# Row standard deviation on one Trainium2 core: another assignment of rows to partitions, single-row loads, and last rows loaded in parts

## The chip, the cores and the metric

One core of one Trainium2 chip runs the kernel; the other cores are idle. Times are device microseconds of one execution, lower is better. A profile's span (first to last instruction) is about 2 us shorter than the time of the same execution. An execution is called slow here when it took over 1.5% more than the fastest one of the same kernel.

DVE is the vector engine and ACT the scalar engine; SP only issues loads and stores. A load is carried out by 16 DMA engines in *packets*; a packet of a load is here the contiguous piece that goes to one partition. A load *lands* when its last byte is in place.

## The reference

```python
x = np.random.randn(8192, 8192).astype(np.float32)     # 268.4 MB

def reference(x):
    return np.std(x, axis=1)                           # 8192 values
```

Each number is read once and used twice, in a sum and in a sum of squares. The variance is (sum of squares - sum^2 / N) / N.

## The kernel before

There are 128 partitions and 8192 rows, so each partition gets 64 rows. Before the change, partition p gets the 64 consecutive rows from 64p on: rows read at the same time by neighbouring partitions lie 64 x 32 KiB = 2 MiB apart. I call that distance the *pitch*. A tile holds two rows of each partition: 8.4 MB, one contiguous piece of 64 KB per partition.

```python
K = 2
T = R // (P * K)                                        # 32 tiles
xv = x.rearrange("(p t k) m -> t p k m", p=P, t=T, k=K)
xpool = ...tile_pool(name="xtiles", bufs=3)
...
for t in range(T):
    xt = xpool.tile([P, K, C], mybir.dt.float32)
    nc.sync.dma_start(out=xt[:], in_=xv[t])             # L39
    nc.vector.reduce_sum(out=allsum[:, t, :], in_=xt[:], axis=...)      # L41, DVE
    for k in range(K):
        for s in range(S):                              # two halves of a row, ACT
            nc.scalar.activation(out=dummy[:], in_=xt[:, k, s*CS:(s+1)*CS],
                                 func=Square, accum_out=allsq[:, t, k, s:s+1])
# after the loop: reduce allsq, square of the sums, subtract (DVE), Sqrt (ACT), one store
nc.sync.dma_start(out=out.rearrange("(p i) -> p i", p=P), in_=std)
```

Of the kernel before, what the change touches and what calls it, by code (L numbers as in the profile page):

```python
# [1 line left out]

# [4 lines left out]


@with_exitstack  # L10
def kernel(
    ctx: ExitStack,
    tc: tile.TileContext,
    x: bass.AP,
    out: bass.AP,
):
    nc = tc.nc
    P = nc.NUM_PARTITIONS
    R, C = x.shape
    K = 2  # L20
    T = R // (P * K)
    S = 2
    CS = C // S
    N = float(C)
    inv_n = 1.0 / N

    xv = x.rearrange("(p t k) m -> t p k m", p=P, t=T, k=K)

    xpool = ctx.enter_context(tc.tile_pool(name="xtiles", bufs=3))
    stats = ctx.enter_context(tc.tile_pool(name="stats", bufs=1))  # L30
    psum = ctx.enter_context(tc.tile_pool(name="psumdump", bufs=1, space=bass.MemoryType.PSUM))

    dummy = psum.tile([P, CS], mybir.dt.float32)
    allsum = stats.tile([P, T, K], mybir.dt.float32)
    allsq = stats.tile([P, T, K, S], mybir.dt.float32)

    for t in range(T):
        xt = xpool.tile([P, K, C], mybir.dt.float32)
        nc.sync.dma_start(out=xt[:], in_=xv[t])  # L39

        nc.vector.reduce_sum(  # L41
            out=allsum[:, t, :],
            in_=xt[:],
            axis=mybir.AxisListType.X,
        )

        for k in range(K):
            for s in range(S):
                nc.scalar.activation(  # L49
                    out=dummy[:],  # L50
                    in_=xt[:, k, s * CS:(s + 1) * CS],
                    func=mybir.ActivationFunctionType.Square,
                    accum_out=allsq[:, t, k, s:s + 1],
                )

    sq = stats.tile([P, T * K], mybir.dt.float32)
    nc.vector.reduce_sum(out=sq, in_=allsq, axis=mybir.AxisListType.X)  # L57

    m2 = stats.tile([P, T * K], mybir.dt.float32)
    nc.vector.scalar_tensor_tensor(  # L60
        out=m2,
        in0=allsum,
        scalar=inv_n,
        in1=allsum,
        op0=mybir.AluOpType.mult,
        op1=mybir.AluOpType.mult,
    )
    nc.vector.tensor_sub(sq, sq, m2)  # L68
    std = stats.tile([P, T * K], mybir.dt.float32)
    nc.scalar.activation(  # L70
        out=std,
        in_=sq,
        func=mybir.ActivationFunctionType.Sqrt,
        scale=inv_n,
    )
    nc.sync.dma_start(out=out.rearrange("(p i) -> p i", p=P), in_=std)


# [1 line left out]
_INS = ['x']  # L80
_OUTS = [((8192,), 'float32')]


# [23 lines left out]
```

## Time and profile before

The time at prediction was 659.8 us (three runs). The profile on which the prediction was made has a span of 662.7 us. Its execution took 664.8 us.

| part of the span | us | what runs |
|---|---|---|
| start | 1.2 | nothing to compute on yet |
| load stream | 641.2 | 32 loads, back to back |
| tail | 20.3 | reduce of the last tile, small operations, store |

From the page of the kernel before: busy time by engine; then, in 40 slices of the span, the busy tenths of the DMA engines and the rate in GB/s; then the costliest group (busy us, mean ns; idle before and what ended it) and the issue line (median us from issue to landing).

```profile
DVE 551.6 (83%) x35; ACT 477.6 (72%) x259; POOL 0.2 (0%) x4
DMA  8999999999999999999999999999999999999950
GB/s 316 340 396 403 396 431 439 388 439 412 407 443 443 439 411 415 443 443 419 415 431 443 443 431 392 443 444 407 415 443 443 443 431 396 439 443 439 392 245 2
L41 DVE TENSOR_REDUCE allsum<-xt 128x2 f32<-128x16384 f32 x32 | 551.0, 17220 | 108.6 <-DMA xt<-in_x_dram 108.6
xt<-in_x_dram SPq DMA_DIRECT2D x32, 41.5
```

The DMA row is 9 from the second slice to the end of the stream, and what ended DVE's idle time is always a load: the kernel is bound by the load stream. Yet the rate is not even. The engines are about as busy in the first two slices as later, but move 316 and 340 GB/s, against 425 on the mean of the other slices of the stream (388 to 444). The same in windows of 21 us (window, its length, busy time and instructions of DVE, ACT and GpSimd, clock, busy share of DMA, GB/s):

```profile
0.00:21.00 21.00, 0.00 (x0) 1.28 (x1) 0.20 (x4) 1.00 0.95 331
21.00:42.00 21.00, 13.58 (x1) 13.49 (x7) 0.00 (x0) 1.00 0.94 346
42.00:63.00 21.00, 15.97 (x2) 13.53 (x9) 0.00 (x0) 1.00 1.02 409
105.00:126.00 21.00, 17.48 (x2) 15.09 (x9) 0.00 (x0) 1.00 1.05 437
```

The chain of waits in order of time (start us, us, what) gives the two ends of the span:

```profile
1.17 49.47 DMA xt<-in_x_dram
67.94 45.04 DMA xt<-in_x_dram
...
601.03 41.32 DMA xt<-in_x_dram
...
642.37 17.22 DVE allsum L41
659.59 0.19 DVE sq L57
```

The chain's second load lands at 67.94 + 45.04 = 113.0 us; it is the fifth of all. The last load lands at 642.4 us. Then DVE spends 17.2 us on a tile on which nothing could start earlier.

### The profile page before, as it was taken

What the parts mean: (1) busy time and instruction counts of PE and PEld (TensorE: products, weight loads), DVE (VectorE), ACT (ScalarE), POOL (GpSimd) and SP (SyncE); (2) the same over time, 40 slices, a digit from 0 to 9 for tenths busy, and PEclk for the clock granted to TensorE, in tenths of its full rate; (3) what the DMA queues carried; (4) which work ended last, traced back from release to release, by engine and by line L of the source; (5) the groups of instructions that cost most, each with busy time, mean ns of one, the idle gap of its engine ahead of it and who ended that gap; (6) DMA issues with size and microseconds to landing.
All of it is one profiled execution on the core that took longest, in us unless ns stands there. A gap on an engine that the chain in (4) does not pass through costs nothing.

```text
span 662.7 us, 432 instructions
## 1 busy us (share of the span) xinstructions
DVE 551.6 (83%) x35; ACT 477.6 (72%) x259; POOL 0.2 (0%) x4
## 2 busy tenths in 40 slices
DVE  0279787898888898888899888889888889988888
ACT  0268666787667788767778777678877777877777
POOL 0000000000000000000000000000000000000000
DMA  8999999999999999999999999999999999999950
GB/s 316 340 396 403 396 431 439 388 439 412 407 443 443 439 411 415 443 443 419 415 431 443 443 431 392 443 444 407 415 443 443 443 431 396 439 443 439 392 245 2
DMA packets 4754, 268.49 MB, mean 405 GB/s; under 512 B 656, under 2 KB 656, under 8 KB 656
## 3 DMA queue, kind: packets, MB, share of 16 engines
q1 hardware_dynamic: 4752, 268.47, 96.2%
q14 instruction: 2, 0.02, 0.0%
HBM read 268.44 MB, written 0.03 MB: 405 GB/s over the span
## 4 chain that ended last, share of the span: by engine, by line
DMA 71%; DVE 29%; issue 0%; SPq 0%; ACT 0%
DMA xt<-in_x_dram 71%; DVE allsum L41 29%; SPq L39 0%; ACT std L70 0%; DVE sq L68 0%; DVE sq L57 0%; DVE m L60 0%
## 5 line engine op out<-in xcount | busy, mean ns | idle before, releaser
L41 DVE TENSOR_REDUCE allsum<-xt 128x2 f32<-128x16384 f32 x32 | 551.0, 17220 | 108.6 <-DMA xt<-in_x_dram 108.6
L49 ACT ACTIVATE dummy<-xt 128x4096 f32<-128x4096 f32 x128 | 459.2, 3587 | 180.6 <-DMA xt<-in_x_dram 177.6
L49 ACT ACTIVATION_READ_ACCUMULATOR dummy<-xt 128x1 f32 x128 | 23.8, 186 | 0.0
L49 ACT ACT_TABLE_LOAD x1 | 1.3, 1283 | 0.7 <-PEq L91 0.7
L70 ACT ACTIVATE std<-sq 128x64 f32<-128x64 f32 x1 | 0.3, 256 | 1.5 <-DVE sq L68 1.5
L70 ACT ACT_TABLE_LOAD x1 | 1.3, 1283 | 0.0
L57 DVE TENSOR_REDUCE sq<-allsq 128x64 f32<-128x128 f32 x1 | 0.3, 276 | 0.0
L68 DVE TENSOR_TENSOR sq<-sq,m 128x64 f32<-128x64 f32 x1 | 0.2, 224 | 0.0
L60 DVE SCALAR_TENSOR_TENSOR m<-allsum 128x64 f32<-128x64 f32 x1 | 0.2, 217 | 0.0
L91 POOL MEMSET const-bfloat16-1.0<- 128x1 bf16 x1 | 0.1, 101 | 0.0
L91 POOL MEMSET const-uint8-127<- 128x1 uint8 x1 | 0.1, 101 | 0.0
L91 POOL MEMSET const-float32-0.0<- 128x1 f32 x1 | 0.1, 98 | 0.2 <-issue 0.2
L91 POOL MEMSET const-float32-1.0<- 128x1 f32 x1 | 0.1, 98 | 0.0
## 6 DMA issues: line engine op xcount, KB each, us to landing
xt<-in_x_dram SPq DMA_DIRECT2D x32, 41.5
out_dram<-std SPq DMA_DIRECT2D x1, 32.0 KB, 1.5
```

Of the source, the lines that this page charges most:

```text
L41: nc.vector.reduce_sum(out=allsum[:, t, :], in_=xt[:], axis=mybir.AxisListType.X,)
L49: nc.scalar.activation(out=dummy[:], in_=xt[:, k, s * CS:(s + 1) * CS], func=mybir.ActivationFunctionType.Square, accum_out=allsq[:, t, k, ...
L57: nc.vector.reduce_sum(out=sq, in_=allsq, axis=mybir.AxisListType.X)
L60: nc.vector.scalar_tensor_tensor(out=m2, in0=allsum, scalar=inv_n, in1=allsum, op0=mybir.AluOpType.mult, op1=mybir.AluOpType.mult,)
L68: nc.vector.tensor_sub(sq, sq, m2)
L70: nc.scalar.activation(out=std, in_=sq, func=mybir.ActivationFunctionType.Sqrt, scale=inv_n,)
L91: nc = _bacc.Bacc("TRN2", target_bir_lowering=False, num_devices=1)
```

## The change

The intent has two parts. The tail: load one row per partition at a time, and the last ten rows in halves and quarters, so that little work is left after the last byte. The layout: group the rows by 16 (`G`), so that the pitch is 16 x 32 KiB = 512 KiB. Further, the results of the first 48 rows are finished early, partly on GpSimd.

```diff
-    xv = x.rearrange("(p t k) m -> t p k m", p=P, t=T, k=K)
+    G = 16
+    xg = x.rearrange("(g p r) m -> g r p m", p=P, r=G)
+    xrows = [xg[i // G, i % G] for i in range(I)]          # I = 64
+    out_pi = out.rearrange("(g p r) -> p g r", p=P, r=G)
+    NB = I - G
+    for i in range(I):
+        n = 1 if i < I - 10 else 2 if i < I - 4 else 4
+        rows.append((i, [C * j // n for j in range(n + 1)]))
-    xpool = ... bufs=3          # tiles of two rows
+    xpool = ... bufs=5          # tiles of one row
...
+    def do_row(i, cuts):
+        xt = xpool.tile([P, C], FP32, name="xt")
+        for ci in range(len(cuts) - 1):
+            c0, c1 = cuts[ci], cuts[ci + 1]
+            nc.sync.dma_start(out=xt[:, c0:c1], in_=xrows[i][:, c0:c1])
+            nc.vector.reduce_sum(out=asum[:, i - base, ci:ci + 1], in_=xt[:, c0:c1], ...)
+            ...  # Square with accum_out, in pieces of at most half a row
...  # after row 47: sums and squares of rows 0 to 47 combined on GpSimd into vA
...  # after row 63: the same for the last 16 rows on DVE into vB
+    stdA = Sqrt(vA);  nc.sync.dma_start(out=out_pi[:, 0:NB // G], in_=stdA...)
+    stdB = Sqrt(vB);  nc.scalar.dma_start(out=out_pi[:, NB // G:], in_=stdB...)
```

More of the change, by code (lines that the diff above doesn't have):

```diff
@@ L7 @@
 from concourse._compat import with_exitstack
+FP32 = mybir.dt.float32
 @with_exitstack
@@ L19 @@
     R, C = x.shape
-    K = 2
-    T = R // (P * K)
-    S = 2
-    CS = C // S
+    I = R // P
     N = float(C)
     inv_n = 1.0 / N
-    xv = x.rearrange("(p t k) m -> t p k m", p=P, t=T, k=K)
-    xpool = ctx.enter_context(tc.tile_pool(name="xtiles", bufs=3))
+    CS = C // 2
+    G = 16
[3 more added lines that the diff above has]
+    NB = I - G
+    rows = []
+    for i in range(I):
+        n = 1 if i < I - 10 else 2 if i < I - 4 else 4
+        rows.append((i, [C * j // n for j in range(n + 1)]))
@@ L30 @@
+    xpool = ctx.enter_context(tc.tile_pool(name="xtiles", bufs=5))
     stats = ctx.enter_context(tc.tile_pool(name="stats", bufs=1))
     psum = ctx.enter_context(tc.tile_pool(name="psumdump", bufs=1, space=bass.MemoryType.PSUM))
-    dummy = psum.tile([P, CS], mybir.dt.float32)
-    allsum = stats.tile([P, T, K], mybir.dt.float32)
-    allsq = stats.tile([P, T, K, S], mybir.dt.float32)
-    for t in range(T):
-        xt = xpool.tile([P, K, C], mybir.dt.float32)
-        nc.sync.dma_start(out=xt[:], in_=xv[t])
-        nc.vector.reduce_sum(
-            out=allsum[:, t, :],
-            in_=xt[:],
-            axis=mybir.AxisListType.X,
-        )
-        for k in range(K):
-            for s in range(S):
+    dummy = psum.tile([P, CS], FP32)
@@ new lines @@
+    NT = I - NB
+    sumA = stats.tile([P, NB, 4], FP32)
+    sqA = stats.tile([P, NB, 4], FP32)
+    sumB = stats.tile([P, NT, 4], FP32)
+    sqB = stats.tile([P, NT, 4], FP32)
+    nc.vector.memset(sumB, 0.0)
+    nc.vector.memset(sqB, 0.0)
+    invn_t = stats.tile([P, 1], FP32)
+    nc.vector.memset(invn_t, inv_n)
+    def do_row(i, cuts):
+        asum, asq, base = (sumA, sqA, 0) if i < NB else (sumB, sqB, NB)
+        xt = xpool.tile([P, C], FP32, name="xt")
+        for ci in range(len(cuts) - 1):
+            c0, c1 = cuts[ci], cuts[ci + 1]
+            nc.sync.dma_start(out=xt[:, c0:c1], in_=xrows[i][:, c0:c1])
+            nc.vector.reduce_sum(
+                out=asum[:, i - base, ci:ci + 1],
+                in_=xt[:, c0:c1],
+                axis=mybir.AxisListType.X,
+            )
+            nsub = (c1 - c0 + CS - 1) // CS
+            step = (c1 - c0) // nsub
+            for si in range(nsub):
+                s0 = c0 + si * step
@@ L49 @@
                 nc.scalar.activation(
-                    out=dummy[:],
-                    in_=xt[:, k, s * CS:(s + 1) * CS],
+                    out=dummy[:, 0:step],
+                    in_=xt[:, s0:s0 + step],
                     func=mybir.ActivationFunctionType.Square,
-                    accum_out=allsq[:, t, k, s:s + 1],
+                    accum_out=asq[:, i - base, ci + si:ci + si + 1],
                 )
-    sq = stats.tile([P, T * K], mybir.dt.float32)
-    nc.vector.reduce_sum(out=sq, in_=allsq, axis=mybir.AxisListType.X)
@@ L59 @@
-    m2 = stats.tile([P, T * K], mybir.dt.float32)
-    nc.vector.scalar_tensor_tensor(
-        out=m2,
-        in0=allsum,
-        scalar=inv_n,
-        in1=allsum,
-        op0=mybir.AluOpType.mult,
-        op1=mybir.AluOpType.mult,
-    )
-    nc.vector.tensor_sub(sq, sq, m2)
-    std = stats.tile([P, T * K], mybir.dt.float32)
-    nc.scalar.activation(
-        out=std,
-        in_=sq,
-        func=mybir.ActivationFunctionType.Sqrt,
-        scale=inv_n,
-    )
-    nc.sync.dma_start(out=out.rearrange("(p i) -> p i", p=P), in_=std)
+    vA = stats.tile([P, NB], FP32)
@@ new lines @@
+    for (i, cuts) in rows:
+        do_row(i, cuts)
+        if i == NB - 1:
+            tsqA = stats.tile([P, NB], FP32)
+            nc.gpsimd.tensor_add(tsqA, sqA[:, :, 0], sqA[:, :, 1])
+            t0 = stats.tile([P, NB], FP32)
+            nc.gpsimd.tensor_mul(t0, sumA[:, :, 0], sumA[:, :, 0])
+            nc.gpsimd.tensor_mul(t0, t0, invn_t.to_broadcast((P, NB)))
+            nc.gpsimd.tensor_sub(vA, tsqA, t0)
+    tsqB = stats.tile([P, NT], FP32)
+    nc.vector.reduce_sum(out=tsqB, in_=sqB, axis=mybir.AxisListType.X)
@@ new lines @@
+    tsumB = stats.tile([P, NT], FP32)
+    nc.vector.reduce_sum(out=tsumB, in_=sumB, axis=mybir.AxisListType.X)
+    m2 = stats.tile([P, NT], FP32)
+    nc.vector.scalar_tensor_tensor(
+        out=m2, in0=tsumB, scalar=inv_n, in1=tsumB,
+        op0=mybir.AluOpType.mult, op1=mybir.AluOpType.mult,
+    )
+    vB = stats.tile([P, NT], FP32)
+    nc.vector.tensor_sub(vB, tsqB, m2)
+    stdA = stats.tile([P, NB], FP32)
+    nc.scalar.activation(out=stdA, in_=vA,
+                         func=mybir.ActivationFunctionType.Sqrt, scale=inv_n)
@@ L80 @@
+    nc.sync.dma_start(out=out_pi[:, 0:NB // G], in_=stdA.rearrange("p (g r) -> p g r", r=G))
+    stdB = stats.tile([P, NT], FP32)
+    nc.scalar.activation(out=stdB, in_=vB,
+                         func=mybir.ActivationFunctionType.Sqrt, scale=inv_n)
+    nc.scalar.dma_start(out=out_pi[:, NB // G:], in_=stdB.rearrange("p (g r) -> p g r", r=G))
 _INS = ['x']
```

## The prediction

> **What bounds the kernel now.** The load stream. In the chain of waits, DMA of xt and the DVE reduce of xt alternate (71% and 29%), but the reduce stands there only because it frees a buffer: a load is issued when a buffer comes free and lands a median 41.5 us later (issue table), about twice its own 19.4 us, so a second one is always queued, and the slices show DMA busy at 9 from the second on. DVE (83%) and ACT (72%) wait for data. The 662.7 us span falls into three parts (chain in order of time, timeline):
> - 0 to 1.2 us: the start.
> - 1.2 to 642.4 us: the stream, 641.2 us for 268.4 MB, 419 GB/s. Its 4096 packets of 64 KB take 2.42 us each once settled (434 GB/s on 16 engines). At that rate it would take 256 x 2.42 = 619 us, so 22 us are lost. 15 us of them go in the first five loads (landed at 113 us, against 97 us plus the start); the windows show 331 and 346 GB/s in the first two 21 us stretches, 409 in the next two, with the engines busy all the same: packets are slower, not fewer.
> - 642.4 to 662.7 us: the tail, 20.3 us: DVE reduces the whole last tile (17.2 us), small operations and sqrt (0.9 us), output DMA (2.2 us).
>
> **What the change does.**
> 1. Tail. The last rows are cut in quarters (128x2048). From 17220 ns for 16384 columns and 276 ns for 128, DVE takes about 2.3 us for one; ACT about 2.1 us, then the table load (1.28 us). Add four small DVE operations (0.8 us), sqrt (0.26 us), output DMA (2.2 us): about 6 us after the last byte. Gain about 14 us, all on the critical path.
> 2. Row layout. The partition pitch in memory falls from 2 MiB to 512 KiB. The Trainium skill, DMA: Bandwidth & Descriptors, section Latency and other measured facts, gives 164 GB/s at 2 MiB, 207 at 512 KiB, 214 when padded, and suspects lock-stepped streams meeting in the same memory channels. 164/214 is 77%; this trace's start is 331/434 = 76%, and the loss fades[...]. No run here shows the 512 KiB case yet; at 97% the first five loads should lose about 3 us. Estimated gain about 12 us.
> 3. Costs. Packets of 32 KB and less (about 10,500): if a packet has some 10 ns of fixed cost, 3 us; small chunks 1 us. Eighty-odd issues of 0.33 us on SP are hidden. DVE needs 8.7 to 9.2 us a row against 9.7 us of DMA, ACT 7.5; five 4 MB buffers leave at least three rows queued.
> 4. GpSimd's part and sqrt of the first 48 rows come before the end, off the path.
>
> **Prediction.** 659.8 - 14.2 - 12 + 3.5: about 637 us, range 629 to 648. Faster by over 2%: 0.85, within 2%: 0.12, slower: 0.03. The floor (stream at 434 GB/s, start, short tail, 2 us outside the span) is about 629 us.
>
> **What would show it right or wrong.** Last load to the end of the span: 5 to 8 us, not 20. First two 21 us windows above 400 GB/s; if they stay near 335, step 2 is wrong and the time is near 648. Settled time per 8.4 MB within 0.3 us of 19.5.
>
> **What could be wrong.** The 512 KiB pitch may keep streams in lock-step longer; small packets may cost more; the chunked loads of one tile might be made to wait for each other's readers, opening gaps in DMA over the last ten rows; the first loads may be slow for another reason than pitch.

## The result

The new kernel takes 635.88 us (median of 12 runs, 635.75 to 636.05). The old one, in 15 runs over several occasions, has a median of 659.67 us (653.79 to 675.07). The ratio of the fast runs is 0.9663 (95% interval 0.9641 to 0.9685): faster by 3.4%. Ratios here are the mean time of one kernel's fast runs over that of the other's of the same rounds, so they are not quite the ratios of the medians quoted. The runs of the new kernel lie within 0.3 us of each other; the 12 fast ones of the old kernel scatter by 7.6 us (653.79 to 661.41), and three more were slow.

The page after, the same lines (DVE's group is now that of the first 48 rows), and the issue line of the last store:

```profile
DVE 558.4 (88%) x89; ACT 480.0 (76%) x276; POOL 1.3 (0%) x8
DMA  8999999999999999999999999999999999999995
GB/s 366 436 432 438 430 432 430 434 430 430 432 432 432 432 430 432 430 430 436 432 430 436 432 429 432 432 432 432 430 436 428 430 430 422 430 429 425 421 422 204
L60 DVE TENSOR_REDUCE sumA<-xt 128x1 f32<-128x8192 f32 x48 | 416.9, 8686 | 61.5 <-DMA xt<-in_x_dram 61.5
xt<-in_x_dram SPq DMA_DIRECT2D x54, 4096.0 KB, 39.8
out_dram<-stdB ACTq DMA_DIRECT2D x1, 8.0 KB, 1.5
```

The windows after:

```profile
0.00:21.00 21.00, 7.72 (x4) 8.70 (x5) 0.20 (x4) 1.00 0.94 389
21.00:42.00 21.00, 18.53 (x3) 14.84 (x8) 0.00 (x0) 1.00 1.00 431
588.00:609.00 21.00, 20.41 (x9) 18.16 (x17) 0.00 (x0) 1.00 1.01 421
```

The chain of waits after, its end:

```profile
608.34 19.90 DMA xt<-in_x_dram
...
628.26 0.03 DVE sumB L60
628.29 2.17 issue
630.46 0.21 DVE tsqB L89
```

The slow start is gone: the second window moves 431 GB/s instead of 346. The rate is flat, and sags to 421 only at the end, where packets are small. The last load lands at 628.2 us, and the span ends 5.9 us later instead of 20.3 us. The "0.03" and "2.17 issue" together are the DVE reduce of the last quarter row.

A profile of an ordinary execution of the old kernel (experiment w1, on another chip) has its last load at 634.6 us and a span of 655.0 us. Against that one, the 20.9 us that the new span is shorter are 14.5 us of tail and 6.4 us of stream. Against the first profile (664.8 us, a slow execution) it would look like 14.4 and 14.1 us; the excess belongs to that slow execution.

### The profile page after: what moved, and what is told of

It reads as the page before. It is cut to its first block, busy times and chain, and to the rows that moved or that the text cites. A ratio compares the mean times of both kernels' runs of the same rounds, so it can differ in the third digit from the quotient of the medians.

```text
span 634.1 us, 643 instructions
## 1 busy us (share of the span) xinstructions
DVE 558.4 (88%) x89; ACT 480.0 (76%) x276; POOL 1.3 (0%) x8
## 4 chain that ended last, share of the span: by engine, by line
DMA 84%; DVE 15%; issue 0%; SPq 0%; ACT 0%
DMA xt<-in_x_dram 84%; DVE sumA L60 14%; DVE sumB L60 1%; SPq L59 0%; ACT stdB L105 0%; DVE tsqB L89 0%; DVE vB L98 0%; DVE m L93 0%; DVE tsumB L91 0%
## 5 line engine op out<-in xcount | busy, mean ns | idle before, releaser
L69 ACT ACTIVATE dummy<-xt 128x4096 f32<-128x4096 f32 (+1 forms) x136 | 460.6, 3386 | 148.8 <-DMA xt<-in_x_dram 146.8
L60 DVE TENSOR_REDUCE sumA<-xt 128x1 f32<-128x8192 f32 x48 | 416.9, 8686 | 61.5 <-DMA xt<-in_x_dram 61.5
L60 DVE TENSOR_REDUCE sumB<-xt 128x1 f32<-128x2048 f32 (+2 forms) x34 | 140.6, 4165 | 10.5 <-DMA xt<-in_x_dram 10.5
L69 ACT ACTIVATION_READ_ACCUMULATOR dummy<-xt 128x1 f32 x136 | 25.3, 186 | 0.0
```

What stands on the lines that cost most here:

```text
L60: nc.vector.reduce_sum(out=asum[:, i - base, ci:ci + 1], in_=xt[:, c0:c1], axis=mybir.AxisListType.X,)
L69: nc.scalar.activation(out=dummy[:, 0:step], in_=xt[:, s0:s0 + step], func=mybir.ActivationFunctionType.Square, accum_out=asq[:, i - base, ...
```

## The experiments

The theory is that the slow start comes from the 2 MiB pitch, and that the gain is the cured stream plus the shorter tail. The rivals: the start was slow because of the large packets or the three 8 MB loads issued at once (*size*); the rows merely lay too far apart (*distance*); the cuts cost in the stream what they save in the tail. "Before" is always the old kernel run beside the experiment on the same chip.

### x1: the new kernel at the old pitch

```diff
-    G = 16
+    G = 64          # pitch 2 MiB; output views adapted
```

> The new kernel with the old row layout: row pitch between partitions 2 MiB again (64 rows), everything else (single rows of 32 KB packets, five buffers, cut last rows) as after the change. Theory pitch: the slow start comes back, the first two 21 us windows read about 330 to 350 GB/s, the time rises by 10 to 15 us to 646 to 651 us and the runs scatter by several us again. Rival size: the start was slow because of 64 KB packets or three 8 MB loads at once; then this stays near 636 us and the first windows above 385 and 430.

Measured: 663.31 us (661.91 to 663.99) beside 653.21 for before, ratio 1.0153 (1.0132 to 1.0174). The expectation missed: it is not 10 to 15 but 27 us slower than the new kernel, and 1.5% slower than the kernel before. The loss also sits elsewhere. Windows of x1:

```profile
0.00:21.00 21.00, 7.12 (x4) 8.18 (x4) 0.20 (x4) 1.00 0.90 356
21.00:42.00 21.00, 17.91 (x3) 15.31 (x10) 0.00 (x0) 1.00 1.00 426
567.00:588.00 21.00, 17.68 (x4) 14.84 (x8) 0.00 (x0) 1.00 1.01 411
588.00:609.00 21.00, 15.69 (x6) 13.46 (x11) 0.00 (x0) 1.00 0.99 296
630.00:651.00 21.00, 11.64 (x6) 10.01 (x10) 0.00 (x0) 1.00 1.01 263
```

The start is nearly healthy (426 in the second window). The halved and quartered rows at the end run at 411, then at 296 and 263 GB/s, with the engines fully busy. The 8 KB packets took 465 ns at the median, against 313 ns after the change. So the pitch does matter, but what it costs depends on how long the pieces are. My reading of the slow start as a property of the pitch alone was too simple.

### x2: the old kernel at the new pitch

```diff
-    xv = x.rearrange("(p t k) m -> t p k m", p=P, t=T, k=K)
+    xg = x.rearrange("(g p t k) m -> g t p k m", p=P, k=K, t=8)   # pitch 512 KiB
+    xv = [xg[t // 8, t % 8] for t in range(T)]
```

> The old kernel (pairs of rows, 64 KB packets, 8 MB loads, three buffers, uncut tail) with the new layout alone, pitch 512 KiB. Theory pitch: stream about 621 us instead of 641, second window above 425 GB/s, time about 644 us with a scatter below 1 us, tail still 20 us. Rival size: time near 659 us and the first windows near 335.

Measured: 646.49 us (646.35 to 646.56), ratio 0.9898 (0.9881 to 0.9916). Windows and the chain's end of x2:

```profile
0.00:21.00 21.00, 0.00 (x0) 1.28 (x1) 0.20 (x4) 1.00 0.94 399
21.00:42.00 21.00, 17.22 (x1) 14.84 (x8) 0.00 (x0) 1.00 1.02 443
```

```profile
582.83 40.74 DMA xt<-in_x_dram
...
623.59 17.22 DVE allsum L43
```

With 64 KB packets, 8 MB loads and three buffers all kept, the slow start vanishes and so does the scatter (four runs within 0.2 us, seven of before within 2.6). The rival *size* falls: large packets alone do no harm. The time is 2.5 us over the expected 644: the stream took 622.4 us instead of 621 and the tail 20.7 instead of 20; the rest is rounding. Beside its own before (653.21), the layout alone is worth 6.7 us. The last load lands at 623.6 us: these 622.4 us are close to the 619 us that 256 packets of 2.42 us per engine need.

### x3: a pitch of 63 rows

Is it the distance, or the power of two? With a pitch of 63 rows (2 MiB less 32 KiB), 63 loads cover the first 8064 rows, and one load takes the last 128.

```diff
-    xg = x.rearrange("(g p r) m -> g r p m", p=P, r=G)          # G = 16
+    G = I - 1
+    xg = x[0:P * G].rearrange("(p r) m -> r p m", p=P)
+    xrows = [xg[i] for i in range(G)] + [x[P * G:]]
```

> The new kernel with a pitch of 63 rows (2 MiB less 32 KiB) for 63 of its 64 loads, and the last 128 rows as one load of pitch one row. Theory aliasing: what hurts is a pitch at a large power of two, so this is as fast as after the change, 635 to 637 us, second window above 425 GB/s. Rival distance: what hurts is that the rows read at one time lie megabytes apart; then it is as slow as with 2 MiB, 646 to 651 us.

Measured: 641.84 us (641.65 to 642.15), ratio 0.9827 (0.9812 to 0.9842). That fits neither number, but the profile parts it cleanly. The chain's end, and the issue lines of the output stores of x3:

```profile
608.20 19.84 DMA xt<-in_x_dram
628.05 0.02 issue
```

```profile
out_dram<-stdB SPq DMA_DIRECT2D x1, 0.5 KB, 6.9
out_dram<-stdB ACTq DMA_DIRECT2D x1, 7.5 KB, 7.6
```

The last load lands at 628.05 us, as after the change (628.24), cut rows included. So rows almost 2 MiB apart are harmless: *distance* falls, and what hurts is a pitch at 2 MiB, or closer to it than 32 KiB. The missing 6 us are in the last stores: their runs are 60 and 4 bytes long here, and the larger landed 7.6 us after issue instead of 1.5. I had not thought of the output. All their packets had ended by 632.4 us, 1.1 us after issue; what the rest was spent on, which of the two stores was at fault, and whether the length of a run or its alignment matters, no run separates.

### x4: no row cut

```diff
-        n = 1 if i < I - 10 else 2 if i < I - 4 else 4
+        n = 1
```

> The new kernel with no row cut into parts. Theory tail: the last landing comes about 1 to 2 us earlier (no 8 KB packets), the tail from last landing to the end grows from 5.9 to about 12.3 us, so the time is about 640.5 to 641.5 us. Rival: the cuts cost in the stream what they save in the tail; then 636 us, with the last landing some 6 us earlier.

Measured: 640.68 us (640.60 to 640.85), as expected. The chain's end of x4:

```profile
586.53 40.50 DMA xt<-in_x_dram
...
627.05 0.04 DVE sumB L60
627.09 8.57 issue
```

Without cuts the last load lands 1.2 us earlier and DVE then needs 6.4 us more. So the cuts are worth 4.8 us (640.68 - 635.88; the spans differ by 5.0), and the rest of the tail's gain, 17.2 - 8.6 = 8.6 us of DVE time, comes from tiles of one row instead of two.

### y1: the old pitch, no row cut

x1 left two readings: the cut rows are what 2 MiB hurts, or the last rows are slow at 2 MiB in any case. y1 is x1 with `n = 1`.

> Pitch 2 MiB and no row cut. The 2 MiB run with cut rows lost 24 us in its last ten rows and only some 2 us at its start. Theory combination: the 8 KB and 16 KB packets of the cut rows are what 2 MiB hurts, so here the end runs at 430 GB/s and the time is 2 to 6 us above the uncut kernel at 512 KiB, 643 to 647 us. Rival place: the last rows are slow at 2 MiB wherever they are cut or not; then the last windows read below 350 GB/s and the time stays above 655 us.

Measured: 644.47 us (643.68 to 645.08) beside 654.20, ratio 0.9844 (0.9814 to 0.9875), as expected. The window from 588 to 609 us, where x1 ran at 296 GB/s:

```profile
588.00:609.00 21.00, 18.94 (x3) 16.40 (x10) 0.00 (x0) 1.00 0.99 428
```

The rival *place* falls. At 2 MiB the cuts turn from a gain of 4.8 us into a loss of 18.8 us (663.31 - 644.47, on two chips).

### y2 and y3: all rows in quarters, at 2 MiB and at 512 KiB

```diff
-        n = 1 if i < I - 10 else 2 if i < I - 4 else 4
+        n = 4           # four parts per row summed in the first 48 rows too
```

> Pitch 2 MiB with all 64 rows cut in quarters (8 KB packets, 256 loads of 1 MB). Theory window: with 8 KB packets all 128 rows are read in the same 8 KB of a 2 MiB stretch, so the collisions never end; the stream runs at 260 to 300 GB/s throughout and the time is 900 to 1030 us. Rival transition: small packets only bring the engines back into step for a while[...]; then the rate recovers to 420 within 100 us and the time is below 700 us.

> The control: pitch 512 KiB with all rows in quarters. At the 313 ns that an 8 KB packet took after the change the stream needs about 641 us, so about 648 to 653 us in all, with windows of 420 GB/s. If small loads by themselves were the trouble (issue, completion, eight loads in flight), this is far slower, towards the 2 MiB case.

Measured: y2 1004.37 us (two runs, 1000.65 and 1008.09), y3 650.66 us (650.65 and 650.66), before 654.20. Two windows of y2, early and late:

```profile
42.00:63.00 21.00, 11.43 (x5) 10.01 (x10) 0.00 (x0) 1.00 0.75 261
903.00:924.00 21.00, 12.44 (x6) 10.80 (x12) 0.00 (x0) 1.00 1.01 259
```

And one of y3:

```profile
567.00:588.00 21.00, 19.18 (x10) 16.63 (x19) 0.00 (x0) 1.00 1.02 423
```

Small packets and 256 loads of 1 MB are fine by themselves: y3 runs at 421 to 423 GB/s. With the 2 MiB pitch the same loads run at about 250 to 290 GB/s from the second window to the last and never recover. So *transition* falls. That the reason is the narrow strip of addresses read at one time is argued, not shown: no run varied the strip at one packet size. Both times lie in their expected ranges. In some windows of y2 the engines are only 0.65 to 0.76 busy; why is open.

### x5: a pitch of 1 MiB

```diff
-    G = 16
+    G = 32
```

> The new kernel, cut rows included, with a pitch of 1 MiB. Theory pitch with a graded effect: between 512 KiB (636 us) and 2 MiB (663 us), about 640 to 655 us, lost in the cut rows. If the effect is a threshold, it equals one of the two ends.

Measured: 637.43 us (637.19 to 637.65), ratio 0.9738 (0.9703 to 0.9773), below the range that I had expected, and with the loss at the start (415 GB/s in the third slice of the page), not in the cut rows. The chain's end of x5:

```profile
609.94 19.86 DMA xt<-in_x_dram
629.80 0.02 issue
```

The last load lands at 629.8 us against 628.2. So 1 MiB costs some 1.5 us with this kernel: of the powers of two that were tried, the large cost appears at 2 MiB and not yet at 1 MiB. It is not a matter of size alone, since 63 rows, nearly 2 MiB, cost nothing in the loads (x3).

### z1, z2, z3: a repeat, contiguous loads, and a version meant to beat both

> The new kernel again, beside the others on one chip: 635.7 to 636.1 us.

Measured: 635.89 us (635.62 to 636.50), ratio 0.9691 (0.9659 to 0.9724). This is the yardstick for the next two, on the same chip. The chain's end of z1:

```profile
608.12 19.89 DMA xt<-in_x_dram
628.01 0.02 issue
```

z2 sets `G = 1`: a pitch of one row, so that each 4 MB load is one contiguous block.

> The new kernel with a pitch of 32 KiB: each 4 MB load is one contiguous block. Theory pitch with a graded effect: no loss in the stream, last load landed at 627.5 to 628.5 us as at 512 KiB. The output then goes out in 4-byte runs; the store of 60-byte runs took 7.6 us at a pitch of 63 rows against 1.5 us, so the tail should grow by more than 5 us and the time be 641 to 650 us. Rival: any power of two as pitch hurts; then the last load lands after 632 us.

Measured: 648.96 us (648.41 to 650.67), ratio 0.9894 (0.9859 to 0.9929). The stream is healthy (429 GB/s in the second window). The page's issue lines for the output of z2:

```profile
out_dram<-stdA SPq DMA_DIRECT2D x1, 24.0 KB, 31.9
out_dram<-stdB ACTq DMA_DIRECT2D x1, 8.0 KB, 12.3
```

The 2048 runs of 4 bytes of the last store landed 12.3 us after issue. The last load's landing is told at 630.6 us, 2.5 us later than in z1, although its last large packet ended at 627.6 us, against 627.5 in z1. The store of the first 48 rows, 6144 runs of 4 bytes, was issued on the same queue 2.5 us after the last load, and its packets ran from about 625 to 636 us; that it delayed the landing is the likely reason, not a tested one. The time lies in the expected range, and the theory's part, no loss in the data packets, holds; the expected landing missed.

z3 joins what x2 and x4 showed: pitch 512 KiB; rows 0 to 43 as 22 pairs with 64 KB packets; then 11 single rows, 6 in halves and 3 in quarters; three buffers of two rows.

```diff
+    for t in range(I // 2):
+        xt = xpool.tile([P, 2, C], FP32, name="xt")              # bufs=3
+        if t < 22:
+            nc.sync.dma_start(out=xt[:], in_=xv[t])              # 64 KB per partition
+            nc.vector.reduce_sum(out=sumA[:, 2*t:2*t+2], in_=xt[:], ...)
+        else: ...      # rows one by one; n = 1 if i < 55 else 2 if i < 61 else 4
```

> A version meant to beat both: pitch 512 KiB, the first 44 rows as 22 pairs with 64 KB packets as in the old kernel, then 11 single rows, 6 halved and 3 quartered. A pair took 19.36 us at 512 KiB in the old kernel against 19.43 us for two single rows in the new, so the stream should end 1.5 to 2 us earlier with the tail still 5.9 us: 633.8 to 634.6 us. If DVE has not caught up by the end, the tail grows and the time is 636 us or more.

Measured: 633.89 us (633.80 to 634.05, five runs), 2.0 us or 0.3% below z1, as expected. Ratio to the old kernel 0.9660 (0.9628 to 0.9692). The chain's end of z3:

```profile
605.84 20.55 DMA xt<-in_x_dram
626.39 0.02 issue
```

The last load lands at 626.4 us (628.0 in z1), and DVE is ready for it. This is the fastest version.

### w1: the old kernel once more

> The old kernel again, for a profile of an ordinary execution: the one profiled first, 664.8 us, is over 1.5% above its fastest. Theory pitch: the slow start is in every execution and only its length varies, so the first two 21 us windows again read 320 to 380 GB/s, the last load lands 630 to 638 us after the start, and the tail is again 20.3 us. If the slow start belonged to that one execution, the windows read above 390 and 430.

Measured: 655.74 us (654.41 and 657.06), the profiled execution a fast one, span 655.0 us. Windows and two lines of the chain of w1:

```profile
0.00:21.00 21.00, 0.00 (x0) 1.28 (x1) 0.20 (x4) 1.00 0.96 350
21.00:42.00 21.00, 15.66 (x1) 14.84 (x8) 0.00 (x0) 1.00 0.99 384
```

```profile
65.16 44.98 DMA xt<-in_x_dram
...
634.63 17.22 DVE allsum L41
```

The slow start (350 and 384 GB/s) is in the ordinary execution too; the second is 4 GB/s above the 380 that I had allowed. The fifth load lands at 110.1 us instead of 113.0. But the start is not all that differs between the two executions: of the 7.7 us between their last loads (634.6 and 642.4), only 2.8 are there at the fifth load, and the rest comes bit by bit later. Beside x2 (on another chip), w1 is 9.7 us behind at the fifth load, 11.7 at the eleventh (228 us) and 11.0 at the last: here the loss ends early. In the slow execution it went on; why is open.

### All of it in one table

Medians in us. The two numbers of the first row were taken on one chip, and so were those of y2 and y3; the others come from several chips, on which before ran at medians of 653.2 to 655.8 us (659.7 where the change was first measured).

| packets of the loads | pitch 2 MiB | pitch 512 KiB | difference |
|---|---|---|---|
| 64 KB (old kernel) | 653.2 | 646.5 (x2) | 6.7 |
| 32 KB, uncut | 644.5 (y1) | 640.7 (x4) | 3.8 |
| 32 KB, last rows 16 and 8 KB | 663.3 (x1) | 635.9 (the change) | 27.4 |
| 8 KB | 1004.4 (y2) | 650.7 (y3) | 353.7 |

Tiles and buffers are the same in the last three rows. From the first row to the second the size of the loads and the number of buffers change together with the packets, so 6.7 against 3.8 us cannot be put down to the packets alone.

## Why the prediction was right, and where it was not

The predicted 637 us with a range of 629 to 648 holds the measured 635.9 us. Point by point:

- *The kernel is bound by the load stream*: right. DMA is busy throughout in all profiles at 512 KiB, and the time follows the stream and the tail.
- *Tail, gain about 14 us*: right. The tail fell from 20.3 to 5.9 us. x4 shows how it splits: cuts 4.8 us net, smaller tiles the rest. One detail was wrong without effect: I counted a table load on ACT after the last square. It was not there; ACT ran the square root of the first 48 rows at 480.5 us, with its table load before it, and the later squares and the last square root needed none.
- *Layout, gain about 12 us*: that the old pitch slows the packets was right (x2); by what mechanism, no run shows. The size is not one number, and it was read from a slow execution. There the fifth 8.4 MB landed at 113.0 us, in an ordinary one (w1) at 110.1, in x2 at 100.4 and after the change at 100.9. The last load of x2 came 18.8 us before that of the slow execution and 11.0 us before that of w1, on another chip; in times on one chip the layout alone gave 6.7 us. The Trainium skill, "DMA: Bandwidth & Descriptors", section "Latency and other measured facts", led to this step with its fall of the rate at 2 MiB and nearly none at 512 KiB; x2 and y3 agree with the latter (no loss to be seen), x3 agrees that it is the power of two.
- *The sum*: 659.8 - 14.2 - 12 + 3.5 came out within 1.2 us, and part of that is luck. With the tail (14.4 us) and the costs (4.6 us) as measured, my estimate of what is left for the layout is 14.1 us from 659.8 to 635.9, but 10 us from the round of z1 (655.84 to 635.89): the old kernel's loss changes with occasion and chip. The new kernel's own time depends less on this: the prediction's floor of 629 us, its costs of 3.5 us and the 3 us that the first loads should still lose make 635.5 us.
- *Costs, about 3.5 us*: close. The last load lands at 623.6 us with 64 KB packets (x2), at 627.0 with 32 KB (x4), at 628.2 with the cuts: 4.6 us. The median packet took 2420 ns at 64 KB (x2), 1218 ns at 32 KB and 313 ns at 8 KB (after), which fits 12 to 15 ns per packet on top of 37.6 ns per KB, against the 10 ns supposed.
- *First two windows above 400 GB/s*: 389 and 431. The first missed, as it holds the 1.2 us of the start and the first packets.
- *Settled time within 0.3 us of 19.5 us per 8.4 MB*: 19.43 us, from the chain's 48.57 us per five rows.
- What the prediction did not see is that its two steps are not independent. It added 14.2 and 12 us. Cuts without the layout cost 18.8 us (x1 against y1). The sum came out because the change does both.

## What to carry to other kernels

Look at the rate at the start and end of a stream apart from its mean: engines that are fully busy at a lower rate have slow packets. Here loads of one row with five buffers made the loss at 2 MiB smaller (3.8 instead of 6.7 us, y1) but did not end it, and still smaller loads made it far worse (y2). Keep the distance between the pieces that the partitions read at one time well below 2 MiB, or off the power of two, above all before loads are cut into small pieces; and then cut only the last ones, as far as the compute engine needs it to catch up. Check that a layout chosen for the loads does not leave the output in runs of a few bytes (64 bytes was the shortest that landed fast here), since a small store at the very end is paid in full.

## What the Trainium skill lacked or had wrong

- "DMA: Bandwidth & Descriptors", section "Latency and other measured facts", gives rates by row pitch for copies with 16 KiB pieces between HBM tensors. For loads into SBUF the effect depends strongly on the piece: at 2 MiB, 8 KB pieces ran at about 250 to 290 GB/s to the end (y2), 64 KB pieces at 331 to 384 GB/s in the first 42 us and at 428 and 432 on the mean after the fifth load (before, w1), and 32 KB pieces lost about 4 us in all (y1). The page has no word on such recovery, nor on the scatter between runs that goes with it (653.8 to 661.4 us in the fast runs).
- The same place gives 207 of 214 GB/s at 512 KiB. Loads here lost nothing that shows: 64 KB packets took 2420 ns at the median at 512 KiB, 2418 in the settled part at 2 MiB, and 32 KB packets 1218 ns at 512 KiB (after), at 63 rows (x3) and contiguous (z2).
- It advises to pad the pitch or to lay tiles out contiguously. Where the tensor cannot be padded, another assignment of rows does the same: a pitch of 63 rows gave the full rate (x3, last load at 628.05 us). Contiguous loads kept the rate too (z2), but made the output's runs 4 bytes long, and the time was 13 us longer (648.96 - 635.89), 10.8 us of it in the landing of the last store.
- The same page, section "Specifications", says that transfers below 512 B are read, modified and written, without a time for small stores. Here 128 runs of 64 B landed in 1.5 us, 128 runs of 60 B beside 128 of 4 B in 7.6 us, and 2048 runs of 4 B in 12.3 us; all of these are below 512 B, so that limit alone does not tell them apart.
- The same page, section "Where 436 GB/s comes from", puts the fabric ceiling at 435 GB/s. The trace agrees: 16 engines with 64 KB in 2.418 us each make 434 GB/s. But it also says that between HBM and SBUF the HBM side binds, at about 358 GB/s; with one core running it did not (434 settled, 423 over the whole span after the change). No run here had a second core loading.
